# A decoder trunk's gated convolution: its input projection in pairs of weight tiles, 7 block products in place of 8

## The chip, the cores and the metric

The kernel runs on one core of a Trainium2 chip. The metric is device time in microseconds, the median of three runs. The engines are named as in the profile: PE (TensorE, matrix products), ACT (ScalarE), DVE (VectorE), POOL (GpSimd) and SP (SyncE, which here issues most of the loads). SBUF is the on-chip memory of 128 partitions; PSUM holds the banks into which PE writes its products, and PE reads only SBUF.

## The reference

One inference step of a trunk of four layers (attention, RG-LRU, gated convolution, attention), each followed by a SwiGLU feed-forward part (FFN). All arithmetic is float32, on 512 prompt tokens and 8 x 8 sample tokens, with a model width of 1024. The part that the change touches is the mixer of the third layer:

```python
def sconv_mixer(h, buf, w_in, conv_w, w_out):        # h = rmsnorm(x, gain)
    bcx = h @ w_in                                   # 1024 -> 3 * 1024
    bg, cg, xv = bcx[..., :D], bcx[..., D:2*D], bcx[..., 2*D:]
    y, new_buf = causal_dwconv(cg * xv, buf, conv_w) # 3 taps along the tokens, per channel
    return (bg * y) @ w_out, new_buf
def rmsnorm(x, g):
    return x * lax.rsqrt(jnp.mean(x * x, axis=-1, keepdims=True) + EPS) * g
def swiglu(h, wg, wu, wd):
    return (jax.nn.silu(h @ wg) * (h @ wu)) @ wd
```

## The kernel before

The tokens lie in two groups g = 0, 1 of 288 columns (256 prompt, 32 sample). x, h and mid are tiles of 8 chunks of 128 channels by 288 tokens for each group. A weight tile is 1024 x 128 and makes one chunk of 128 outputs. For float32 exactness each operand is held as a rounded high part and a remainder (hh and hl, wh and wl, mh and ml), and a product of one 128-channel chunk is three matmuls of 288 columns: hh with wh, hl with wh, hh with wl (mm3, lines 439 to 441). A unit is one weight tile times one group: 8 chunks, 24 matmuls. ACT makes wh from the raw tile (a cast), DVE makes wl (a subtraction), in wprep (lines 359 and 361), out of 4 raw buffers into 6 slots.

A Python scheduler (class Sched) with a cost for each operation fixes the order of the instructions on each engine when the program is built. Each engine then works through its own list in that order, and waits where an operand is not there yet. The cost table has one price for each operation, whatever runs beside it.

The mixers multiply h = x * gain (gsplit, line 473) and bring the norm's factor r in when the product leaves PSUM, so PE can start on a chunk of x as soon as it is there. In the gated convolution cg_evac multiplies by r squared (line 1237), the taps' result is multiplied by r (line 1261). For each of 8 chunks c the tiles cg, xv and bg follow one another, each for both groups: 24 tiles, 48 units. xv_evac forms cg * xv into ext (lines 1247, 1249), POOL writes the halos (halos, lines 1017 to 1023), conv does the three taps on DVE (lines 1038 to 1048), bg_evac multiplies by bg and splits the result into mh and ml (lines 468, 470).

The FFN already does its first projection in another way, from its fourth tile pair on (quad, inside ffn): gate and up tile of a pair, each cut in two halves along the inner axis, and the two token groups form a 2 x 2 block product, done with 7 products of half a tile (12 matmuls each) in place of 8. For that h must be exactly normed (hsplit, line 486, after the norm's factor is known), sums of the four token blocks (T1 to T4, tsums) are made once for the layer, and for each pair four sums of weight halves S1 to S4 (qsums, lines 378 to 388) - on DVE for the first NEAR = 2 pairs of a layer, on POOL after that. Each of the 7 half tiles gets its cast on ACT (line 412) and its subtraction on DVE (line 414). The product banks are partly reused: ACT copies a bank out (snap) before the next product is accumulated into it, and DVE adds the copy to another bank (lines 1343, 1380).

Of the kernel before, what the change touches and what calls it, by code (L numbers as in the profile page):

```python
# [8 lines left out]
F32 = mybir.dt.float32  # L9
# [4 lines left out]
P = 128  # L14
D = 1024
# [22 lines left out]
NEAR = 2  # L38
NSTP = 1
# [214 lines left out]
class Builder(Sched):  # L254
# [136 lines left out]
    def qprep(self, i):  # L391
        layer, last = self.quads[i]
# [89 lines left out]
    def hsplit(self, g, m, idx):  # L482

        hh, hl = (t[:, m, :] for t in self.h[g])
        keep = g == 1 or m < KC // 2
        if g == 0 and keep:
            yield ("wait", [("ffnlp", idx // 2)])
# [115 lines left out]
    def rstd(self, g, idx, ps, w1):  # L603
# [14 lines left out]
        if idx % 2:  # L618
# [591 lines left out]

    def sconv(self, layer):
        nc = self.nc
# [4 lines left out]
        def enter():  # L1217
            self.open(layer)
            lt = self.lt
            cr = lt("cr", [P, 384])  # L1220
            nc.gpsimd.dma_start(out=cr, in_=self.a["cr"])
            st["sst"] = self.pick(cr, CR, "sst")
# [3 lines left out]
            st["ext"] = Pool([(lt(f"ext{i}", [P, w]), lt(f"cv{i}", [P, w])) for i in range(3)])  # L1226
            st["u"] = Pool([lt(f"u{i}", [P, N]) for i in range(8)])
            st["r2"] = [lt(f"rr{g}", [P, N]) for g in range(2)]

        def cg_evac(g, c, ps):  # L1230
            [t] = yield ("acq", st["u"], 1)
            yield ("wait", [("r", g, idx)])
            if c == 0:
                yield ("D", cD(N, 1))
                nc.vector.tensor_mul(st["r2"][g], self.rt[g], self.rt[g])
            yield ("D", cD(N, 1))
            nc.vector.tensor_mul(t, ps[:, :N], st["r2"][g])
# [4 lines left out]
        def xv_evac(g, c, ps):  # L1242
# [4 lines left out]
            nc.vector.tensor_mul(ext[:, 2:2 + NP], u[:, :NP], ps[:, :NP])  # L1247
            yield ("D", cD(NS))
            nc.vector.tensor_mul(self.sview(ext, S0, SS)[:, :, 2:SS], u[:, NP:].rearrange("p (b t) -> p b t", t=T),
                                 ps[:, NP:N].rearrange("p (b t) -> p b t", t=T))  # L1250
            yield ("free", self.pp, [ps])
# [8 lines left out]
            yield ("D", cD(N))  # L1260
            nc.vector.tensor_mul(u, u, self.rt[g])
            yield ("set", ("cu", g, c))

        def bg_evac(g, c, ps):
# [3 lines left out]
            nc.vector.tensor_mul(u, u, ps[:, :N])  # L1268
            yield ("free", self.pp, [ps])
# [4 lines left out]

        self.hook(6, enter)
        for c in range(KC):
            for ev in (cg_evac, xv_evac, bg_evac):
                i = self.take()
                for g in range(2):
                    self.add(g, lambda prio, i=i, g=g, c=c, ev=ev: self.unit(  # L1280
                        i, g, self.h, self.hkeys(g, idx), lambda ps: ev(g, c, ps)))
        self.mixed = [("mc", g, c) for g in range(2) for c in range(KC)] + [("out", layer)]
# [9 lines left out]
    def ffn(self, layer):  # L1292
# [6 lines left out]
        hk = KC // 2  # L1299
        T = {}  # L1300
        mixed = self.mixed

        def enter():
            yield ("wait", mixed)
            self.open(f"{layer}f")
            for n in ("T2", "T1", "T3", "T4"):
                T[n] = tuple(self.lt(n + s, [P, hk, N], F32R) for s in "hl")
            self.stp = Pool([tuple(self.lt(f"S{j}{i}", [P, HW]) for j in range(2)) for i in range(NSTP)])
            self.b11 = [self.lt(f"b11{i}", [P, N]) for i in range(hk)]
            self.qseen = []  # L1310
            yield ("set", ("ffnlp", layer))

        def tsums(k):
            yield ("wait", [("h", g, idx, m) for g in range(2) for m in (k, k + hk)])
            b11, b12, b22 = (self.whole.pop(gm) for gm in ((0, k), (1, k), (1, k + hk)))
            hh, hl = (a[:, k + hk, :].bitcast(F32) for a in self.h[0])
            [t4] = yield ("acq", self.scr, 1)
            sub, add = nc.vector.tensor_sub, nc.vector.tensor_add
            for n, t, x, y, op in (("T1", b11, b12, b11, sub), ("T3", b12, b22, b12, sub), ("T2", b22, b22, b11, sub),
                                   (None, t4, hh, b22, sub), ("T4", t4, t4, hl, add)):  # L1320
                yield ("D", cD(N))
                op(t, x, y)

            def parts(n, t):
                yield from self.split(T[n][0][:, k, :], T[n][1][:, k, :], t, N, 1)
            for n, t in (("T1", b11), ("T3", b12), ("T2", b22), ("T4", t4)):
                yield ("spawn", parts(n, t), None, [("T", layer, n, k)])
            yield ("wait", [("T", layer, n, k) for n in ("T1", "T3", "T2", "T4")])
            yield ("free", self.scr, [b12, b22, t4])
# [23 lines left out]
        def quad(i, s, m, lst):  # L1353
            key = lambda g: (layer, s, g, m)
            h = lambda g, z: [a[:, z * hk:(z + 1) * hk, :] for a in self.h[g]]
            hkeys = lambda g, z: [("h", g, idx, m) for m in range(z * hk, (z + 1) * hk)]
            tkeys = lambda n: [("T", layer, n, k) for k in range(hk)]
            add = nc.vector.tensor_add
            c = {}

            def prod(n, ps, x, first, last):
                slot, wh, wl = self.qh.pop((i, n))
                yield ("P", 0.369 * hk, None, None, 864 * hk)
                xh, xl = x
                mm = nc.tensor.matmul
                for k in range(hk):
                    mm(ps[:, :N], lhsT=wh[:, k, :], rhs=xh[:, k, :], start=first and k == 0, stop=False, skip_group_check=not first)  # L1367
                    mm(ps[:, :N], lhsT=wh[:, k, :], rhs=xl[:, k, :], start=False, stop=False, skip_group_check=not first)  # L1368
                    mm(ps[:, :N], lhsT=wl[:, k, :], rhs=xh[:, k, :], start=False, stop=k == hk - 1, skip_group_check=not first)  # L1369
                yield from self.usehalf(slot)  # L1370

            def snap(n, ps):
                [c[n]] = yield ("acq", self.scr, 1)
                yield ("A", cA(N))
                nc.scalar.copy(c[n], ps[:, :N])
                yield ("set", ("c", i, n))

            def plus(t, ps):
                yield ("D", cD(N))
                add(t, t, ps[:, :N])  # L1380

            def silu(t):
                yield ("A", cA(N, 1), None, "silu")
                nc.scalar.activation(out=t, in_=t, func=AF.Silu)  # L1384

            def gate0():
                yield ("wait", [("c", i, 1)])
                yield from plus(c[1], b)
                yield ("free", self.pp, [b])
                yield from silu(c[1])  # L1390
                yield ("set", ("gs", i))

            def up1():
                yield ("wait", [("c", i, 5)])
                yield from plus(c[5], a)
                yield ("set", ("u", i))

            def gate1():
                yield from plus(c[2], d)
                yield ("free", self.pp, [d])  # L1400
                yield from silu(c[2])
                yield ("wait", [("u", i)])
                yield ("D", cD(N))
                nc.vector.tensor_mul(c[2], c[2], c[5])
                yield ("free", self.scr, [c[5]])
                yield from done(1, key(1), m, c[2])

            yield ("wait", [("qw", i, "A11")] + hkeys(0, 0))
            [a] = yield ("acq", self.pp, 1)
            yield from prod("A11", a, h(0, 0), True, False)  # L1410
            yield ("spawn", snap(1, a), None, [])
            yield ("wait", [("qw", i, "A12")] + hkeys(0, 1))
            [b] = yield ("acq", self.pp, 1)
            yield from prod("A12", b, h(0, 1), True, True)
            yield ("spawn", gate0(), None, [])
# [260 lines left out]
```

## Time and profile before

| | |
|---|---|
| median of 3 runs | 2353.8 us (2353.73 to 2353.94) |
| the profiled execution | 2353.24 us; its span, first to last instruction, is 2351.3 us |
| granted TensorE clock, mean | 0.998 |
| PE busy | 2324.0 us, 99% of the span |
| DVE busy | 1672.2 us, 71% |
| ACT busy | 1226.6 us, 52% |
| POOL busy | 542.6 us, 23% |

A row of the timeline has the start (us from the span's start), the duration, engine, line, operation and operands, and in brackets the idle time before it with what ended it. Consecutive instructions of one engine overlap a little in such records, so the cost of one in a full queue is read from start to start. The gated convolution's mixer stands between 1161 us (the norm's matmul of group 0 before it) and 1363 us (that of the FFN behind it).

### The profile page before, as it was taken

What the parts mean: (1) busy time and instruction counts of PE and PEld (TensorE: products, weight loads), DVE (VectorE), ACT (ScalarE), POOL (GpSimd) and SP (SyncE); (2) the same over time, 40 slices, a digit from 0 to 9 for tenths busy, and PEclk for the clock granted to TensorE, in tenths of its full rate; (3) what the DMA queues carried; (4) which work ended last, traced back from release to release, by engine and by line L of the source; (5) the groups of instructions that cost most, each with busy time, mean ns of one, the idle gap of its engine ahead of it and who ended that gap; (6) DMA issues with size and microseconds to landing.
All of it is one profiled execution on the core that took longest, in us unless ns stands there. A gap on an engine that the chain in (4) does not pass through costs nothing.

```text
span 2351.3 us, 44296 instructions
## 1 busy us (share of the span) xinstructions
PE 2324.0 (99%) x17596; PEld 2295.5 (98%) x17596; DVE 1672.2 (71%) x3315; ACT 1226.6 (52%) x2545; POOL 542.6 (23%) x636
## 2 busy tenths in 40 slices
PE   9999999999999999999999999999999999999998
PEld 8899999999999999999999999999999899999998
DVE  8978848486886885848665578484868959757474
ACT  8955625255695653525422256252548945535353
POOL 2300334240231033323000003242402400333330
PEclk9999999999999999999999999999999999999999
DMA  5111323233222132323322213232242111323131
GB/s 189 61 57 47 112 87 99 73 101 102 72 82 93 52 122 66 113 72 101 97 85 82 83 55 98 93 98 81 88 138 83 56 46 54 126 73 110 62 109 49
DMA packets 64064, 203.69 MB, mean 87 GB/s; under 512 B 11041, under 2 KB 13905, under 8 KB 63841
## 3 DMA queue, kind: packets, MB, share of 16 engines
q1 hardware_dynamic: 62800, 199.52, 26.7%
q8 instruction: 138, 2.26, 0.4%
q10 hardware_dynamic: 720, 0.73, 0.1%
q0 software_dynamic: 336, 0.61, 0.1%
q14 instruction: 70, 0.57, 0.1%
HBM read 197.87 MB, written 4.94 MB: 86 GB/s over the span
## 4 chain that ended last, share of the span: by engine, by line
PE 86%; ACT 6%; DVE 4%; issue 2%; DMA 1%; POOL 0%; DVEq 0%; ACTq 0%
PE bank L439 16%; PE bank L440 16%; PE bank L441 16%; PE bank L1367 12%; PE bank L1369 12%; PE bank L1368 12%; ACT s L753 2%; ACT wh L359 1%; DVE P L841 1%; PE bank L890 1%; PE bank L906 1%; ACT P L847 0%; DVE P L855 0%; ACT PT L892 0%; DVE wl L361 0%
## 5 line engine op out<-in xcount | busy, mean ns | idle before, releaser
L439 PE MATMUL bank<-mh,wh 128*128 128x288 f32 x1984 | 589.2, 297 | 1.7 <-ACT mh L468 1.7
L440 PE MATMUL bank<-ml,wh 128*128 128x288 f32 x1984 | 586.0, 295 | 0.5 <-DVE ml L470 0.4
L441 PE MATMUL bank<-mh,wl 128*128 128x288 f32 x1984 | 583.7, 294 | 0.0
L439 PE MATMUL bank<-hh,wh 128*128 128x288 f32 x1344 | 404.1, 301 | 4.1 <-ACT s L1123 1.5
L440 PE MATMUL bank<-hl,wh 128*128 128x288 f32 x1344 | 397.3, 296 | 0.0
L441 PE MATMUL bank<-hh,wl 128*128 128x288 f32 x1344 | 396.3, 295 | 0.0
L414 DVE TENSOR_TENSOR wl<-raw,wh 128x512 fp32r<-128x512 f32 x380 | 375.9, 1011 | 22.8 <-ACT wh L412 22.6
L359 ACT CAST wh<-raw 128x1024 fp32r<-128x1024 f32 (+2 forms) x217 | 219.0, 1014 | 326.0 <-PE bank L440 213.1
L439 PEld LDWEIGHTS bank<-mh,wh 128*128 128x128 f32 x1984 | 371.9, 187 | 3.4 <-ACT mh L468 2.5
L440 PEld LDWEIGHTS bank<-ml,wh 128*128 128x128 f32 x1984 | 372.5, 188 | 1.8 <-DVE ml L470 1.3
L441 PEld LDWEIGHTS bank<-mh,wl 128*128 128x128 f32 x1984 | 373.7, 188 | 0.0
L361 DVE TENSOR_TENSOR wl<-raw,wh 128x1024 fp32r<-128x1024 f32 (+2 forms) x217 | 256.7, 1183 | 65.9 <-ACT wh L359 64.0
L655 DVE TENSOR_TENSOR x<-bank,x 128x288 f32<-128x288 f32 x224 | 101.9, 457 | 280.1 <-PE bank L441 279.9
L412 ACT CAST wh<-raw 128x512 fp32r<-128x512 f32 x380 | 229.5, 619 | 95.2 <-PE bank L440 94.6
L1367 PE MATMUL bank<-hh,wh 128*128 128x288 f32 x912 | 270.0, 296 | 0.0
L1368 PE MATMUL bank<-hl,wh 128*128 128x288 f32 x912 | 269.1, 295 | 0.0
L1369 PE MATMUL bank<-hh,wl 128*128 128x288 f32 x912 | 268.2, 294 | 0.0
L439 PEld LDWEIGHTS bank<-hh,wh 128*128 128x128 f32 x1344 | 252.5, 188 | 6.7 <-ACT s L1123 1.7
L440 PEld LDWEIGHTS bank<-hl,wh 128*128 128x128 f32 x1344 | 253.1, 188 | 0.8
L441 PEld LDWEIGHTS bank<-hh,wl 128*128 128x128 f32 x1344 | 253.7, 189 | 0.1
L1384 ACT ACTIVATE s<-s 128x288 f32<-128x288 f32 x152 | 67.8, 446 | 216.7 <-DVE s L1380 215.6
L1369 PEld LDWEIGHTS bank<-hh,wl 128*128 128x128 f32 x912 | 171.9, 188 | 0.0
(382 smaller groups left out, 4863.9 us busy)
## 6 DMA issues: line engine op xcount, KB each, us to landing
raw<-in_w SPq DMA_DIRECT2D x303, 512.0 KB
raw<-in_w SPq DMA_DIRECT2D x64, 448.0 KB
out_y<-x SPq DMA_DIRECT2D x12, 144.0 KB
x<-in_x SPq DMA_DIRECT2D x4, 288.0 KB
x<-in_x SPq DMA_DIRECT2D x2, 576.0 KB
ck<-in_ckt SPq DMA_DIRECT2D x4, 256.0 KB
cv<-in_cv SPq DMA_DIRECT2D x4, 256.0 KB
ca<-in_ca SPq DMA_DIRECT2D x2, 480.0 KB
```

The source lines that it names most:

```text
L359: self.nc.scalar.copy(fh[:, z], r[:, z])
L361: self.nc.vector.tensor_sub(fl[:, z], r[:, z], fh[:, z].bitcast(F32))
L412: self.nc.scalar.copy(fh, src)
L414: self.nc.vector.tensor_sub(fl, src, fh.bitcast(F32))
L439: mm(out, lhsT=wh(k), rhs=xh(k), start=(k == 0), stop=False)
L440: mm(out, lhsT=wh(k), rhs=xl(k), start=False, stop=False)
L441: mm(out, lhsT=wl(k), rhs=xh(k), start=False, stop=(k == n - 1))
L655: nc.vector.tensor_add(x[:, m, :], ps[:, :N], x[:, m, :])
L1367: mm(ps[:, :N], lhsT=wh[:, k, :], rhs=xh[:, k, :], start=first and k == 0, stop=False, skip_group_check=not first)
L1368: mm(ps[:, :N], lhsT=wh[:, k, :], rhs=xl[:, k, :], start=False, stop=False, skip_group_check=not first)
L1369: mm(ps[:, :N], lhsT=wl[:, k, :], rhs=xh[:, k, :], start=False, stop=k == hk - 1, skip_group_check=not first)
L1384: nc.scalar.activation(out=t, in_=t, func=AF.Silu)
```

## The change

Only the gated convolution layer changes. x is exactly normed before its projection (hsplit in place of gsplit; BLOCKED names the norms that do this), so that r and r squared go out of the evacuations. The first two chunks stay as units (the copy out of PSUM for cg is now on ACT). From the third chunk on two tiles that share their inputs are taken as a pair: (cg, xv) of a chunk, and the bg tiles of two chunks (S_ORDER; the packed weights are reordered to match). Each such pair is a quad of 7 products; there are 9. The FFN's quad, tsums and the tiles T1 to T4 become methods that both use, with what is done with the four results handed in: for (cg, xv) the products and taps, for (bg, bg) the gating. The T1 tiles of this layer lie in chunks 6 and 7 of mid, which are needed last. Two pairs of ext buffers are there in place of three, and three u tiles in place of eight.

```diff
+BLOCKED = (1, 3, 4, 5, 7)
+SPRE = 2
+S_ORDER = []
+for _c in range(KC):
+    if _c < SPRE:
+        S_ORDER += [(1, _c), (2, _c), (0, _c)]
+    elif (_c - SPRE) % 2:
+        S_ORDER += [(1, _c - 1), (2, _c - 1), (1, _c), (2, _c), (0, _c - 1), (0, _c)]
...
-        if idx < 2 * self.layers and idx % 2 == 0:
+        if idx < 2 * self.layers and idx not in BLOCKED:
             yield ("spawn", self.gsplit(g, m, idx), GOFF, [("h", g, idx, m)])
...
-        if idx % 2:
+        if idx in BLOCKED:
             for m in range(KC):
                 yield ("spawn", self.hsplit(g, m, idx), GOFF + 0.01 * m, [("h", g, idx, m)])
...
+    def tsums(self, k, idx, done=None):        # moved out of ffn
...
+        for n, t, x, y, op in (("T1", b11, b12, b11, sub), ("T3", b12, b22, b12, sub), ("T2", b22, b22, b11, sub),
+                               (None, t4, hh, b22, sub), ("T4", t4, t4, hl, add)):
+            yield ("D", cD(N))
+            op(t, x, y)
...
+    def quad(self, i, lst, idx, dest, first, second):
...
+        def snap(n, ps):
+            [c[n]] = yield ("acq", self.scr, 1)
+            yield ("A", cA(N))
+            nc.scalar.copy(c[n], ps[:, :N])
+            yield ("set", ("c", i, n))
+
+        def head(g, n, ps):
+            t = yield from dest(g, c[n])
+            yield ("D", cD(N))
+            add(t, c[n], ps[:, :N])
...
+        def tail1():
+            yield ("wait", [("c", i, 5)])
+            yield ("D", cD(N))
+            add(c[5], c[5], a[:, :N])
+            yield ("set", ("u", i))
...
     def sconv(self, layer):
...
-            st["ext"] = Pool([(lt(f"ext{i}", [P, w]), lt(f"cv{i}", [P, w])) for i in range(3)])
-            st["u"] = Pool([lt(f"u{i}", [P, N]) for i in range(8)])
-            st["r2"] = [lt(f"rr{g}", [P, N]) for g in range(2)]
+            st["ext"] = Pool([(lt(f"ext{i}", [P, w]), lt(f"cv{i}", [P, w])) for i in range(2)])
+            st["u"] = Pool([lt(f"u{i}", [P, N]) for i in range(3)])
+            self.blocks(idx, [lambda k, s=s: self.mid[k // 2][s][:, KC - 2 + k % 2, :] for s in range(2)])
...
         def cg_evac(g, c, ps):
...
-            nc.vector.tensor_mul(t, ps[:, :N], st["r2"][g])
+            yield ("A", cA(N))
+            nc.scalar.copy(t, ps[:, :N])
...
             yield from self.conv(u, ext, t, 3, "scw", None, c)
             yield ("free", st["ext"], [(ext, t)])
-            yield ("D", cD(N))
-            nc.vector.tensor_mul(u, u, self.rt[g])
...
+            self.add_quad(i, lst, idx, not order, *(cgxv(c) if part else bgbg(c)))
```

On DVE, in the gated convolution: this is the piece between two weight tiles in the program before, for one chunk, with a group's taps (L1038 to L1048), the multiplication by r (L1261), the gating (L1268) and two whole-tile wl (L361). wl_80 and ext_2_11866 are buffers with their numbers.

```order
L1247 TENSOR_TENSOR ext_2_11866<-u_2_11868,bank_61 128x256
L1249 TENSOR_TENSOR ext_2_11866<-u_2_11868,bank_61 128x4x8
L361 TENSOR_TENSOR wl_80<-raw_71,wh_79 128x1024
L1038 TENSOR_SCALAR cv_2_11867<-ext_2_11866,cpack 128x296
L1042 SCALAR_TENSOR_TENSOR cv_2_11867<-ext_2_11866,cpack,cv_2_11867 128x296
L1046 SCALAR_TENSOR_TENSOR u_2_11868<-ext_2_11866,cpack,cv_2_11867 128x256
L1048 SCALAR_TENSOR_TENSOR u_2_11868<-ext_2_11866,cpack,cv_2_11867 128x32
L1261 TENSOR_TENSOR u_2_11868<-u_2_11868,rt_108 128x288
L1268 TENSOR_TENSOR u_2_11875<-u_2_11875,bank_62 128x288
L470 TENSOR_TENSOR ml_103<-u_2_11875,mh_102 128x288
L1268 TENSOR_TENSOR u_2_11868<-u_2_11868,bank_66 128x288
L361 TENSOR_TENSOR wl_76<-raw_72,wh_75 128x1024
```

The same place in the changed program, inside a (cg, xv) quad: half-tile wl (L422), the additions of bank and copy (L1299, L1314), and the taps of both groups (L1046 to L1056) drawn together.

```order
L422 TENSOR_TENSOR wl_84<-S_2_11875,wh_83 128x512
L1299 TENSOR_TENSOR u_2_11866<-s_94,bank_67 128x288
L1046 TENSOR_SCALAR cv_2_11863<-ext_2_11862,cpack 128x296
L1046 TENSOR_SCALAR cv_2_11865<-ext_2_11864,cpack 128x296
L1050 SCALAR_TENSOR_TENSOR cv_2_11863<-ext_2_11862,cpack,cv_2_11863 128x296
L1050 SCALAR_TENSOR_TENSOR cv_2_11865<-ext_2_11864,cpack,cv_2_11865 128x296
L1054 SCALAR_TENSOR_TENSOR u_2_11867<-ext_2_11862,cpack,cv_2_11863 128x256
L1056 SCALAR_TENSOR_TENSOR u_2_11867<-ext_2_11862,cpack,cv_2_11863 128x32
L1054 SCALAR_TENSOR_TENSOR u_2_11868<-ext_2_11864,cpack,cv_2_11865 128x256
L1056 SCALAR_TENSOR_TENSOR u_2_11868<-ext_2_11864,cpack,cv_2_11865 128x32
L422 TENSOR_TENSOR wl_80<-raw_70,wh_79 128x512
L1314 TENSOR_TENSOR s_85<-s_85,bank_61 128x288
```

Whole-tile subtractions have become half-tile ones between which the additions and the taps stand; the multiplication by r is gone.

On POOL, in the gated convolution before: the halos of two groups stand directly one behind the other, and nothing else is there.

```order
L1017 MEMSET ext_2_11866 128x2
L1018 COPY halo_11859<-ext_2_11866 128x2
L1022 COPY ext_2_11866<-cr_11857 128x4x2
L1023 COPY outs_11861<-ext_2_11866 128x8
L1020 COPY ext_2_11862<-halo_11859 128x2
```

And now: the four sums of weight halves of a pair (L386 to L396, with the scratch S and the raw tiles) stand between the halos of one chunk and the next.

```order
L386 TENSOR_TENSOR S_2_11875<-raw_70 128x512
L389 TENSOR_TENSOR S_2_11876<-S_2_11875,raw_69 128x512
L392 TENSOR_TENSOR raw_70<-raw_69,raw_70 128x512
L396 TENSOR_TENSOR raw_69<-raw_69,S_2_11876 128x512
L1025 MEMSET ext_2_11862 128x2
L1026 COPY halo_11859<-ext_2_11862 128x2
L1030 COPY ext_2_11862<-cr_11857 128x4x2
L1031 COPY outs_11861<-ext_2_11862 128x8
```

28 such sums (7 pairs of 4) have come to POOL; the first two pairs have theirs on DVE.

## Rows read from the trace of the kernel before

**Rows 1.** The page: busy time, share of the span and instructions of each engine
```profile
PE 2324.0 (99%) x17596; PEld 2295.5 (98%) x17596; DVE 1672.2 (71%) x3315; ACT 1226.6 (52%) x2545; POOL 542.6 (23%) x636
```
**Rows 2.** Windows: stretch, its length, busy us (instructions) of PE, PEld, DVE, ACT, POOL, clock, DMA
```profile
1163.00:1363.00 200.00, 200.00 (x1500) 199.90 (x1500) 114.04 (x228) 47.36 (x69) 10.31 (x65) 1.00 0.27 84
1390.00:1410.00 20.00, 20.00 (x152) 20.00 (x152) 19.21 (x47) 11.01 (x27) 0.00 (x0) 1.00 0.01 2
1543.00:1554.00 11.00, 11.00 (x85) 11.00 (x84) 10.02 (x15) 6.38 (x15) 5.96 (x4) 1.00 0.34 93
```
**Rows 3.** Timeline of PE in an FFN quad, two rows 48 matmuls apart
```profile
1099.82 0.30 PE L1367 MATMUL bank<-hh,wh 128*128 128x288 f32 x1
...
1106.22 0.30 PE L1367 MATMUL bank<-T3h_1f,wh 128*128 128x288 f32 x1
```
**Rows 4.** Timeline of PE and DVE at the norm before the gated convolution, group 0
```profile
1161.42 0.65 PE L600 MATMUL bank<-s,ones 128*128 128x288 f32 x2
...
1162.04 0.29 PE L440 MATMUL bank<-hl,wh 128*128 128x288 f32 x1
...
1163.02 0.46 DVE L613 SCALAR_TENSOR_TENSOR s<-bank,s 128x288 f32<-128x288 f32 x1 [1.23 <-ACT s L610]
```
**Rows 5.** Timeline of DVE in the FFN behind, while its T sums are made
```profile
1395.65 0.46 DVE L1322 TENSOR_TENSOR s<-s,b_2f 128x288 f32<-128x288 f32 x1
1396.14 0.46 DVE L1322 TENSOR_TENSOR s<-hh,s 128x288 f32<-128x288 f32 x1
...
1397.38 0.68 DVE L414 TENSOR_TENSOR wl<-raw,wh 128x512 fp32r<-128x512 f32 x1
1397.98 0.45 DVE L470 TENSOR_TENSOR T1l_2f<-b_2f,T1h_2f 128x288 fp32r<-128x288 f32 x1
1398.35 0.45 DVE L470 TENSOR_TENSOR T3l_2f<-s,T3h_2f 128x288 fp32r<-128x288 f32 x1
```
**Rows 6.** Timeline of DVE in the gated convolution: one group's product and taps, one whole-tile wl
```profile
1244.95 0.42 DVE L1247 TENSOR_TENSOR ext<-u,bank 128x256 f32<-128x256 f32 x1 [0.97 <-PE bank L441]
1245.29 0.18 DVE L1249 TENSOR_TENSOR ext<-u,bank 128x32 f32<-128x32 f32 x1
1245.79 0.38 DVE L1038 TENSOR_SCALAR cv<-ext,cpack 128x296 f32<-128x296 f32 x1 [0.31 <-POOL ext L1022]
...
1247.44 0.46 DVE L1261 TENSOR_TENSOR u<-u,rt 128x288 f32<-128x288 f32 x1
...
1249.15 1.23 DVE L361 TENSOR_TENSOR wl<-raw,wh 128x1024 fp32r<-128x1024 f32 x1 [0.48 <-ACT wh L359]
1250.29 0.37 DVE L1038 TENSOR_SCALAR cv<-ext,cpack 128x296 f32<-128x296 f32 x1
```
**Rows 7.** Timeline of DVE and POOL in one FFN quad
```profile
1545.52 4.57 DVE L414 TENSOR_TENSOR wl<-raw,wh 128x512 fp32r<-128x512 f32 x3
1550.01 0.44 DVE L1380 TENSOR_TENSOR s<-s,bank 128x288 f32<-128x288 f32 x1
...
1553.44 1.15 DVE L414 TENSOR_TENSOR wl<-S_2f,wh 128x512 fp32r<-128x512 f32 x1
1554.52 0.82 DVE L470 TENSOR_TENSOR ml<-s,mh 128x288 fp32r<-128x288 f32 x2
...
1544.83 1.29 POOL L378 TENSOR_TENSOR S_2f<-raw 128x512 f32<-128x512 f32 x1 [1.97 <-DVE wl L414]
...
1552.67 1.38 POOL L388 TENSOR_TENSOR raw<-raw,S_2f 128x512 f32<-128x512 f32 x1 [3.13 <-DVE wl L414]
```
**Rows 8.** By source line: instructions, duration ns min/median/max, first and last start, forms
```profile
L414 DVE TENSOR_TENSOR wl<-raw,wh x380: 677/685/1802, 218.4 to 2278.1; 128x512 fp32r<-128x512 f32 x190
...
L748 DVE SCALAR_TENSOR_TENSOR s<-s,cpack,cos x36: 497/514/987, 25.6 to 1878.6; 128x288 f32<-128x288 f32 x36
```
**Rows 9.** Timeline of DVE and POOL in the first attention layer
```profile
57.88 0.98 DVE L748 SCALAR_TENSOR_TENSOR s<-s,cpack,cos 128x288 f32<-128x288 f32 x1
...
57.68 0.86 POOL L830 TENSOR_TENSOR ml<-s,ml 64x256 fp32r<-64x256 f32 x1
```

More of the change, by code (lines that the diff above doesn't have):

```diff
@@ L391, in qprep @@
     def qprep(self, i):
-        layer, last = self.quads[i]
+        last = self.quads[i][1]
         for j, n in enumerate(("A11", "A12", "S2", "S1", "S3", "S4", "A22")):
@@ L486, in hsplit @@
         if g == 0 and keep:
-            yield ("wait", [("ffnlp", idx // 2)])
+            yield ("wait", [("lpq", idx)])
             t = self.b11[m]
@@ L1209, in rglru, with blocks @@
         self.spawn(outputs(), 1e6, 0.0, [("out", layer)])
+    def blocks(self, idx, t1=None):
+        hk = KC // 2
+        T = self.T = {}
+        for n in ("T2", "T1", "T3", "T4"):
+            if n == "T1" and t1 is not None:
+                T[n] = t1
+            else:
+                T[n] = [lambda k, t=self.lt(n + s, [P, hk, N], F32R): t[:, k, :] for s in "hl"]
+        self.stp = Pool([tuple(self.lt(f"S{j}{i}", [P, HW]) for j in range(2)) for i in range(NSTP)])
+        self.b11 = [self.lt(f"b11{i}", [P, N]) for i in range(hk)]
+        self.qseen = []
+        self.set(("lpq", idx), 0.0)
@@ L1267, in bg_evac @@
             yield ("D", cD(N))
-            nc.vector.tensor_mul(u, u, ps[:, :N])
-            yield ("free", self.pp, [ps])
+            nc.vector.tensor_mul(u, u, x)
+            if ps is not None:
+                yield ("free", self.pp, [ps])
+            if c >= KC - 2:
+                yield ("wait", [("pd", st["last"], "S1")])
             mh, ml = self.mid[g]
@@ L1273, in bg_evac, with cgxv, dest, first @@
             yield ("set", ("mc", g, c))
-        self.hook(6, enter)
-        for c in range(KC):
-            for ev in (cg_evac, xv_evac, bg_evac):
+        def cgxv(c):
+            def dest(g, t):
+                [u] = yield ("acq", st["u"], 1)
+                return u
+            def first(g, t):
+                st["cg", g, c] = t
+                yield ("set", ("cg", g, c))
+            def second(g, t, x, ps=None):
+                yield from xv_evac(g, c, x, ps)
+            return dest, first, second
+        def bgbg(c):
+            def dest(g, t):
+                return t
+                yield
+            def first(g, t):
+                yield ("spawn", one(g, t), None, [])
+            def one(g, t):
+                yield from bg_evac(g, c, t)
+                yield ("free", self.scr, [t])
+            def second(g, t, x, ps=None):
+                yield from bg_evac(g, c + 1, x, ps)
+            return dest, first, second
+        self.hook(6, enter)
+        tprio = self.nunits[1] + TOFF
+        lst = 0
+        order = list(S_ORDER)
+        while order:
+            part, c = order[0]
+            if c < SPRE:
+                order.pop(0)
                 i = self.take()
+                ev = (lambda g, c, ps: bg_evac(g, c, ps[:, :N], ps), cg_evac,
+                      lambda g, c, ps: xv_evac(g, c, ps[:, :N], ps))[part]
                 for g in range(2):
@@ L1281, in sconv @@
                         i, g, self.h, self.hkeys(g, idx), lambda ps: ev(g, c, ps)))
+                continue
+            order = order[2:]
+            i = self.take()
+            self.take()
+            st["last"] = i
+            self.add_quad(i, lst, idx, not order, *(cgxv(c) if part else bgbg(c)))
+            lst ^= 1
         self.mixed = [("mc", g, c) for g in range(2) for c in range(KC)] + [("out", layer)]
@@ L1305, in enter, with silu @@
             self.open(f"{layer}f")
[L1306 to L1329, printed above, removed]
+            self.blocks(idx)
+        def silu(t, x):
+            yield ("A", cA(N, 1), None, "silu")
+            nc.scalar.activation(out=t, in_=x, func=AF.Silu)
         def gate_evac(g, key, ps):
             [t] = yield ("acq", self.scr, 1)
-            yield ("A", cA(N), None, "silu")
-            nc.scalar.activation(out=t, in_=ps[:, :N], func=AF.Silu)
+            yield from silu(t, ps[:, :N])
             yield ("free", self.pp, [ps])
@@ L1351, in done @@
             yield ("set", ("mf",) + key)
[L1353 to L1415, printed above, removed]
-            yield ("wait", [("qw", i, "S2"), ("c", i, 1)] + tkeys("T2"))
-            yield from prod("S2", a, T["T2"], False, False)
-            yield ("spawn", snap(2, a), None, [])
-            yield ("wait", [("qw", i, "S1")] + tkeys("T1"))
-            [d] = yield ("acq", self.pp, 1)
-            yield from prod("S1", d, T["T1"], True, False)
-            yield ("spawn", snap(5, d), None, [])
-            yield ("wait", [("qw", i, "S3"), ("c", i, 2)] + tkeys("T3"))
-            yield from prod("S3", a, T["T3"], False, False)
-            yield ("spawn", up1(), None, [])
-            yield ("wait", [("qw", i, "S4"), ("c", i, 5)] + hkeys(1, 1))
-            yield from prod("S4", d, h(1, 1), False, True)
-            yield ("spawn", gate1(), None, [])
-            yield ("wait", [("qw", i, "A22"), ("u", i)] + tkeys("T4"))
-            yield from prod("A22", a, T["T4"], False, True)
-            self.open_quads -= 1
-            self.next_unit(lst, self.t["P"])
-            yield ("wait", [("gs", i)])
-            yield ("D", cD(N))
-            nc.vector.tensor_mul(c[1], c[1], a[:, :N])
-            yield ("free", self.pp, [a])
-            yield from done(0, key(0), m, c[1])
@@ L1439, in start_quad, with pair, dest, first @@
-        def start_quad(prio, i, s, m, lst):
-            self.open_quads += 1
-            return quad(i, s, m, lst)
+        def pair(s, m):
+            def dest(g, t):
+                return t
+                yield
+            def first(g, t):
+                yield from silu(t, t)
+            def second(g, t, x, ps=None):
+                yield from times(g, (layer, s, g, m), m, t, x, ps)
+            return dest, first, second
         self.spawn(enter(), 0.0, 0.0)
-        for k in range(hk):
-            self.spawn(tsums(k), self.nunits[1] + TOFF + 0.1 * k, 0.0)
+        for k in range(KC // 2):
+            self.spawn(self.tsums(k, idx), self.nunits[1] + TOFF + 0.1 * k, 0.0)
@@ L1457, in ffn @@
                     continue
-                self.quads[i] = (layer, m == ns - 1)
-                lst = (m - pre) % 2
-                self.units[lst].append((i + QOFF, lambda prio, i=i, s=s, m=m, lst=lst: start_quad(prio, i, s, m, lst)))
-                for g in range(2):
-                    self.nunits[g] += 2
+                self.add_quad(i, (m - pre) % 2, idx, m == ns - 1, *pair(s, m))
             last = s == len(SEGS) - 1
@@ L1549, in _weights @@
             w = i["sconv_w_in"][0]
-            for c in range(8):
-                out += [_mt(w, _cols(8 + c)), _mt(w, _cols(16 + c)), _mt(w, _cols(c))]
+            out += [_mt(w, _cols(8 * part + c)) for part, c in S_ORDER]
             out += [_mt(i["sconv_w_out"][0], _cols(m)) for m in range(8)]
```

124 lines of the change are left out of this document (102 added, 22 removed).

## The prediction

> **What bounds the kernel now.** I read the page first: PE is busy 99% of the span, DVE 71%, POOL 23% [rows 1]. That is an average, so I went on to windows over the gated convolution's mixer, from one norm to the next: in 200 us PE is never idle, DVE is busy 114 us and POOL 10 us [rows 2]. No wait of PE stands there, so matmuls taken out of this stretch shorten the run one for one, as long as the other engines keep up. The timeline of PE gives the price: 48 matmuls from 1099.82 to 1106.22, so 0.1333 us each, inside an FFN quad as in a unit [rows 3]. The other two windows show what DVE looks like where the trick is already used: 19.21 of 20 us while the FFN norms h and makes its T sums, 10.02 of 11 us in a quad, PE full in both [rows 2]. So DVE is the engine to count. In a full queue one DVE instruction follows the other before the record of the first ends: a 128x288 one costs 0.37 us, a half-tile wl 0.60, a dependent one behind another 0.49 [rows 5]; a whole-tile wl 1.14 [rows 6].
>
> **The change part by part.**
>
> *PE.* 9 quads take 84 matmuls where 4 units took 96: 108 matmuls less, 14.4 us. That is the whole gain if PE stays full: 2338.8 from the profiled execution's 2353.24 us.
>
> *The later start of h.* The projection now waits for the norm. PE fills the time with the last out-products of group 1: in the new order 63 matmuls (8.4 us) stand between the norm's matmul and the first product with hh of group 0. From that matmul DVE needs 1.6 us to reach the norm's first instruction [rows 4], then some 9 us to the eighth chunk (two norm instructions, a whole-tile wl, eight products of 0.43, which lies between the 0.37 and 0.49 of rows 5, eight remainders of 0.37, two others). The first chunk is there after about 6 us, the eighth at about 10.6, and PE asks for it 84 matmuls (11.2 us) after the norm. It fits; I cost it at nothing. Without that cover it would be about 2 us once.
>
> *DVE, the sum that decides.* In the new order PE has 1108 matmuls from group 0's norm to the first out-product: 147.7 us. Two norm matmuls cost 0.35 us extra each (0.62 us from rows 4 less two of 0.1333). The first out-product needs chunk 7 of mid only at its 22nd matmul, 2.8 us in. Less 0.2 us for the hand-over, DVE has 151.0 us. In that time it has to do, in its order: 63 half-tile wl x 0.605 = 38.1; 48 remainders (h, T, mid) x 0.37 = 17.8; 20 T sums x 0.45 = 9.0 (some dependent, some not); 16 normings x 0.43 = 6.9; 27 additions of a copy and a bank x 0.37 = 10.0; 16 products cg * xv x 0.44 = 7.0 (0.34 to the second part [rows 6] and 0.10 for that); taps of 16 chunks, 4 alone x 1.65 [rows 6] and 12 drawn together, where the three dependent waits of 0.12 (0.49 less 0.37) go away, x 1.29: 22.1; 16 gatings x 0.37 = 5.9; 5 whole-tile wl for the out-projection x 1.14 = 5.7; the weight sums of the first two pairs, 8 x 0.62 = 5.0; some 3.9 for two norms and the end of the last adds. Sum 131.4 us, with the 1.6 us of the start 133.0. By that DVE would be done 18 us early, and this is also what an order with one fixed price for each operation assumes.
>
> *What the fixed price leaves out.* In the FFN quad three wl take 4.49 us from start to start of what follows, in place of 1.82, and one takes 1.08 in place of 0.60: together 3.1 us more in a quad, just while POOL makes that quad's four sums [rows 7]. So a POOL sum costs DVE 0.79 us there. The longest wl is 1802 ns against a median of 685 [rows 8]: 1.12 us is the price of one full collision. An addition that reads a bank is not stretched (0.44 us beside the sums) [rows 7]. In the FFN quad the sums fall partly into DVE's idle time and beside those additions. In the gated convolution's quads there is hardly idle time, and the taps are no cover either: L748, which like a tap has two tiles in SBUF, takes 0.98 us beside a POOL sum, its median is 0.51 [rows 8, 9]. Only the additions and half of the products read PSUM, about 5 of 24 instructions of a quad. 28 sums have come to POOL. No row shows a sum beside a full DVE: the bounds are 0 (every sum beside something that reads PSUM) and 28 x 1.12 = 31.4 us. I take 0.92 each, between the quad's 0.79 and the full 1.12: 25.8 us.
>
> The Trainium skill, page "SBUF — State Buffer", section "Who interferes with whom", says that a DVE instruction with two SBUF inputs and a GpSimd instruction that reads SBUF exclude each other, and that the second waits for the whole of the first. The trace agrees for wl and for L748. Taken strictly, the rule gives about 1.1 us for each sum, a loss some 5 us above mine, and 2356.
>
> *Small waits of DVE.* POOL's halos now stand behind sums of 1.3 to 1.4 us [rows 7], the taps wait for the halos, the remainders for ACT's casts. In the dense 20 us of the FFN 0.8 us were idle [rows 2], 4%. Over 150 us that would be 6; part of it is in the sum already (dependent spacing). I take 4, bounds 0 and 12.
>
> *The sum.* 133.0 + 25.8 + 4 = 162.8 us of DVE against 151.0: PE loses 11.8 us of the 14.4 to waits for wl and for the last ml. Net 2.6 us faster than the profiled execution, 2350.6; the median of the runs stood 0.6 above it, so 2351.2.
>
> *What costs nothing.* ACT has 88 more rows in its order, copies and half-tile casts; from 47 us busy in 200 [rows 2] it goes to some 90 in 148, below DVE. The r products that go (16 of 0.37 and 18 that leave or go to ACT) are already missing from the list above. SP loads the same bytes. After the out-products begin DVE has only 51 us of PE work with 3 more whole-tile wl and the adds beside it, so nothing is carried into the FFN.
>
> **The rivals.**
>
> *PE stays full.* If the sums cost DVE at most 0.5 us each (14 us), DVE needs 133.0 + 14 + 2 = 149 us and PE loses nothing: 2353.24 - 14.4 + 0.6 = 2339.4. At the quad's 0.79 (22 us) and 2 us of small waits the loss is 6 us, and the time 2345.5. For it: the FFN's quads run at 10 of 11 us with PE full [rows 2]. Against it: the (cg, xv) quad has 4.6 us of additions, products and taps besides its 4.2 us of wl; with 3 to 4 us of collisions that is about 12.3 in PE's 11.2.
>
> *Slower.* Each collision costs the full 1.12 (31.4 us), and because POOL, itself held up, delivers halos and sums late, DVE waits 12 us more: 133.0 + 31.4 + 12 = 176 us, a loss of 25, so 2353.24 + 11 + 0.6 = 2365. It turns slower than before from a loss of 14.4 us on, that is from 32.4 us of collisions and waits together; I have 29.8. For it: POOL's queue now mixes short urgent copies with sums. Against it: the order leaves 2 to 4 us of other DVE work between a product in ext and its taps.
>
> *The change brings no fewer products.* Excluded: the new order has 108 matmuls less, and rows 3 show the same pace in a quad.
>
> **How the numbers follow.** A run tells 0.2%, 4.7 us, from no change: faster is below 2349.1, slower above 2358.5. The forecast is DVE as the limit with a loss of 10 to 19 us, within the 0.2% (2349 to 2358): 0.42. PE full or nearly so, a loss up to 10 us: 0.34. Slower, a loss beyond 19: 0.24. The predicted time is 2351.2, in the middle of what 0.79 to 1.12 us per sum give with 2 to 6 us of small waits (2345 to 2359). The range leaves out the two ends, full PE and the worst queueing: 2341 to 2361.
>
> **What would show it.** Right: the quads of this layer show PE waiting for wl by DVE, mostly from the third pair on, DVE above 9.5 of 10 us there, wl beside POOL sums at 1.1 to 1.8 us, and 10 to 14 us idle in PE. The start: no PE wait between norm and first product with hh. Wrong: PE without idle time in the quads (then the collisions hide beside the taps, and L1050 or L1054 show no stretch); or DVE idle for more than 10 us waiting on POOL or ACT; or PE waiting for ACT's copies of banks, which I have at nothing.

## The result, and the profile after

The changed kernel takes 2369.6 us (2368.3 to 2370.7), the one before 2353.8 (2353.0 to 2353.9): ratio 1.0068, interval 1.0055 to 1.0080. It is 15.8 us slower; 2351.2 was predicted, in a range of 2341 to 2361. The 108 matmuls and their 14.4 us are gone, so some 30 us were lost. From the FFN's norm behind the layer to the end both kernels take 988 us, so the loss stands in the changed layer.

The page, and the windows from the norm's matmul of group 0 to the last product with h (in the kernel before such a stretch is the first window of [rows 2]). Columns as there.

```profile
PE 2320.1 (98%) x17488; PEld 2288.1 (97%) x17488; DVE 1726.1 (73%) x3413; ACT 1257.9 (53%) x2637; POOL 586.6 (25%) x664
```
```profile
1159.24:1338.30 179.06, 159.56 (x1115) 156.36 (x1113) 152.38 (x307) 73.26 (x158) 54.89 (x93) 0.94 0.21 63
...
1290.65:1295.40 4.75, 4.75 (x24) 4.75 (x25) 1.98 (x5) 0.00 (x0) 0.00 (x0) 0.64 0.43 117
```

PE, full before, is idle for 19.5 of these 179 us, and the mean clock is 0.94. But DVE is not full either: 152.4 us busy, 26.7 idle. In the old kernel such idle time of DVE was harmless; here two engines wait for each other. The views of waits show for what (who waited <- for whom, us in total, times, longest):

```profile
PE bank L1286 <- DVE wl L422: 18.6, 7, 4.5
PE bank L448 <- DVE hl L478: 0.6, 2, 0.3
PE bank L447 <- ACT hh L476: 0.3, 1, 0.3
...
DVE s L1314 <- PE bank L1286: 8.7, 7, 1.7
DVE s L1299 <- PE bank L1286: 5.3, 5, 1.5
DVE u L1299 <- PE bank L1286: 3.7, 4, 1.7
DVE b L1299 <- PE bank L1286: 3.2, 3, 1.5
DVE x L663 <- PE bank L449: 2.0, 2, 1.3
DVE wl L422 <- ACT wh L420: 1.3, 2, 1.1
...
DVE cv L1046 <- POOL ext L1030: 0.4, 2, 0.2
```

PE waits 18.6 us for wl in 7 waits; four of 3.1 to 4.6 us stand in the quads 3, 5, 6 and 8, each time at the first matmul that needs S3's wl (T3h with wl). DVE waits 20.9 us in 19 waits for a bank that PE has still to finish. For POOL's halos it hardly waits.

One of the four, the (bg, bg) quad, in the timelines of PE, DVE, ACT and POOL:

```profile
1285.68 0.29 PE L1284 MATMUL bank<-T3h,wh 128*128 128x288 f32 x1
1285.81 0.29 PE L1285 MATMUL bank<-T3l,wh 128*128 128x288 f32 x1
...
1290.65 0.45 PE L1286 MATMUL bank<-T3h,wl 128*128 128x288 f32 x1 [4.55 <-DVE wl L422]
1290.90 0.44 PE L1284 MATMUL bank<-T3h,wh 128*128 128x288 f32 x1
1291.14 0.44 PE L1285 MATMUL bank<-T3l,wh 128*128 128x288 f32 x1
```
```profile
1282.75 0.46 DVE L1299 TENSOR_TENSOR s<-s,bank 128x288 f32<-128x288 f32 x1 [1.55 <-PE bank L1286]
1283.12 0.70 DVE L422 TENSOR_TENSOR wl<-S,wh 128x512 fp32r<-128x512 f32 x1
1283.74 0.45 DVE L1409 TENSOR_TENSOR u<-u,s 128x288 f32<-128x288 f32 x1
1284.11 1.41 DVE L1046 TENSOR_SCALAR cv<-ext,cpack 128x296 f32<-128x296 f32 x1
1285.55 1.47 DVE L1050 SCALAR_TENSOR_TENSOR cv<-ext,cpack,cv 128x296 f32<-128x296 f32 x1
1286.94 1.38 DVE L1046 TENSOR_SCALAR cv<-ext,cpack 128x296 f32<-128x296 f32 x1
1288.24 0.47 DVE L1054 SCALAR_TENSOR_TENSOR u<-ext,cpack,cv 128x256 f32<-128x256 f32 x1
...
1289.91 0.68 DVE L422 TENSOR_TENSOR wl<-raw,wh 128x512 fp32r<-128x512 f32 x1
```
```profile
1281.89 0.62 ACT L420 CAST wh<-raw 128x512 fp32r<-128x512 f32 x1
...
1283.90 1.44 POOL L386 TENSOR_TENSOR S<-raw 128x512 f32<-128x512 f32 x1 [0.63 <-DVE wl L422]
1285.42 1.28 POOL L389 TENSOR_TENSOR S<-S,raw 128x512 f32<-128x512 f32 x1
1286.65 1.49 POOL L392 TENSOR_TENSOR raw<-raw,raw 128x512 f32<-128x512 f32 x1
```

Read from the top of DVE's list. It is early and stands idle 1.55 us before an addition whose bank PE has not finished; the cast of S3 is there at 1282.51, before DVE goes on, but its subtraction stands further back. First come the wl of S1, a gating, and the eight tap instructions of both groups, and only then the wl of S3, which PE wants at 1285.95. The same wl of S1 sets POOL going: it frees the one pair of scratch tiles S, and the next pair's three sums run back to back just beside the taps, where three of DVE's instructions take 1.38 to 1.47 us in place of 0.36 to 0.53. PE stops for 4.55 us, and its next 15 matmuls come 0.24 us apart, at a granted clock of 0.64 in the window above (the lower of the two levels, 1.2 GHz, for most of it). Behind the four stops the trace has 66 matmuls at that spacing, 0.107 us more each than in [rows 3]: 7.1 us.

### The profile page after: what moved, and what is told of

Read it like the earlier page. It is cut to its first block, busy times and chain, and to the rows that moved or that the text cites. A ratio compares the mean times of both kernels' runs of the same rounds, so it can differ in the third digit from the quotient of the medians.

```text
span 2368.6 us, 44341 instructions
## 1 busy us (share of the span) xinstructions
PE 2320.1 (98%) x17488; PEld 2288.1 (97%) x17488; DVE 1726.1 (73%) x3413; ACT 1257.9 (53%) x2637; POOL 586.6 (25%) x664
## 4 chain that ended last, share of the span: by engine, by line
PE 84%; ACT 7%; DVE 6%; issue 2%; POOL 0%; DMA 0%; DVEq 0%; ACTq 0%
PE bank L447 14%; PE bank L449 14%; PE bank L448 14%; PE bank L1284 13%; PE bank L1286 13%; PE bank L1285 13%; ACT s L761 2%; ACT wh L367 1%; DVE cv L1050 1%; PE bank L898 1%; DVE wl L369 1%; PE bank L914 1%; DVE wl L422 1%; DVE P L849 0%; ACT P L855 0%
## 5 line engine op out<-in xcount | busy, mean ns | idle before, releaser
L422 DVE TENSOR_TENSOR wl<-raw,wh 128x512 fp32r<-128x512 f32 x425 | 411.0, 987 | 24.2 <-ACT wh L420 24.0
L367 ACT CAST wh<-raw 128x1024 fp32r<-128x1024 f32 (+2 forms) x199 | 200.0, 1009 | 241.3 <-PE bank L448 156.4
L447 PE MATMUL bank<-hh,wh 128*128 128x288 f32 x1056 | 318.1, 301 | 4.4 <-ACT s L1131 1.5
L448 PE MATMUL bank<-hl,wh 128*128 128x288 f32 x1056 | 311.9, 295 | 0.6 <-DVE hl L478 0.6
L449 PE MATMUL bank<-hh,wl 128*128 128x288 f32 x1056 | 310.9, 294 | 0.0
L420 ACT CAST wh<-raw 128x512 fp32r<-128x512 f32 x425 | 255.3, 619 | 95.3 <-PE bank L448 94.7
L1284 PE MATMUL bank<-hh,wh 128*128 128x288 f32 x1020 | 303.7, 298 | 0.0
L1285 PE MATMUL bank<-hl,wh 128*128 128x288 f32 x1020 | 302.6, 297 | 0.0
L1286 PE MATMUL bank<-hh,wl 128*128 128x288 f32 x1020 | 301.6, 296 | 0.2 <-DVE wl L422 0.2
L369 DVE TENSOR_TENSOR wl<-raw,wh 128x1024 fp32r<-128x1024 f32 (+2 forms) x199 | 235.4, 1183 | 53.4 <-ACT wh L367 51.3
L447 PEld LDWEIGHTS bank<-hh,wh 128*128 128x128 f32 x1056 | 198.1, 188 | 7.3 <-ACT s L1131 1.8
L448 PEld LDWEIGHTS bank<-hl,wh 128*128 128x128 f32 x1056 | 198.4, 188 | 1.7 <-DVE hl L478 1.0
L449 PEld LDWEIGHTS bank<-hh,wl 128*128 128x128 f32 x1056 | 198.7, 188 | 0.2 <-DVE wl L369 0.2
L1286 PEld LDWEIGHTS bank<-hh,wl 128*128 128x128 f32 x1020 | 193.8, 190 | 0.6 <-DVE wl L422 0.4
L1285 PEld LDWEIGHTS bank<-hl,wh 128*128 128x128 f32 x1020 | 193.2, 189 | 0.0
```

The source lines that it names most:

```text
L367: self.nc.scalar.copy(fh[:, z], r[:, z])
L369: self.nc.vector.tensor_sub(fl[:, z], r[:, z], fh[:, z].bitcast(F32))
L420: self.nc.scalar.copy(fh, src)
L422: self.nc.vector.tensor_sub(fl, src, fh.bitcast(F32))
L447: mm(out, lhsT=wh(k), rhs=xh(k), start=(k == 0), stop=False)
L448: mm(out, lhsT=wh(k), rhs=xl(k), start=False, stop=False)
```

## Experiments

Theory O: the order does it, DVE idle before an addition and then a block in front of the wl that PE needs. Theory C: the collisions with POOL's sums do it, as predicted, only larger. Of each experiment one number is also read in its trace: how DVE's time from the norm to the last product with h divides.

**a1, the taps ranked later.** In the scheduler a lower number goes first. With i the number of a pair's first weight tile, the wl of its S3 has i + 0.14 (L418); the taps inherit the rank of the quad two weight tiles earlier, i - 0.25. The expectation puts the stops at 23 us and the lower clock at 8.7; the views above give 19.5 and 7.1.

```diff
-            yield ("spawn", taps(g, c, u, ext, t), None, [("cu", g, c)])
+            yield ("spawn", taps(g, c, u, ext, t), 2.0, [("cu", g, c)])
```


> Same work as the changed kernel, all products and sums; only the taps get a lower rank in the scheduler (offset 2.0), so that on DVE the weight remainders of the following quad stand ahead of them. Theory O (order): PE loses its 23 us of stops and 8.7 us at the lower clock because the taps of both groups stand in DVE's list just ahead of the remainder for S3 that PE asks for next. Then the four stops of 3.4 to 4.8 us at the T3 products go, and with them the low clock behind them: 2344 to 2351 us. Theory C (collisions, as I predicted, only larger): DVE simply has too little time, since POOL's 28 sums hold it up; the same work in another order loses the same, with the stops elsewhere: 2364 to 2372.

Measured 2355.0 us, ratio to before 1.0008 (0.9999 to 1.0018): 14.6 us of the changed kernel's time are gone with the same work in another order. The windows' row:

```profile
1158.84:1322.90 164.06, 153.69 (x1115) 149.06 (x1114) 156.10 (x305) 73.34 (x156) 55.61 (x93) 1.00 0.23 71
```

DVE is busy 156.1 us, as before this edit and even a little more, but idle only 8.0 in place of 26.7, and the clock is whole. PE still loses time, now in many short stops of up to 1.5 us. O holds for this half. The time is 4 us above O's range, so O is not all.

**b1, the sums made narrow.** The order is unchanged.

```diff
+        m = HW if near or self.quads[i][0] != 4 else 16
-        pl.tensor_add(s1, u[:, :HW], u[:, HW:])
+        pl.tensor_add(s1[:, :m], u[:, :m], u[:, HW:HW + m])
```


> The changed kernel's order, instruction for instruction; POOL's 28 sums of weight halves in the gated convolution are made on 16 of 512 columns, so this layer's result is not the reference's. Theory C: without the sums nothing holds DVE up, the stops go altogether: 2338 to 2344 us, no stop over 0.5 us at the T3 products. Theory O: the taps still stand ahead of S3's remainder; only their stretch of some 2.5 to 3 us goes, so four stops of 1 to 2.2 us stay at the T3 products, too short to bring the clock down: 2346 to 2353.

Measured 2349.9 us, 0.9984 (0.9975 to 0.9994), 19.7 less than the changed kernel. DVE's row, and PE at the place shown above:

```profile
1159.23:1317.70 158.47, 151.39 (x1114) 148.82 (x1113) 132.44 (x307) 73.18 (x157) 23.69 (x93) 1.00 0.23 71
```
```profile
1277.77 0.40 PE L1287 MATMUL bank<-T3h,wl 128*128 128x288 f32 x1 [1.56 <-DVE wl L423]
1278.01 0.30 PE L1285 MATMUL bank<-T3h,wh 128*128 128x288 f32 x1
1278.15 0.30 PE L1286 MATMUL bank<-T3l,wh 128*128 128x288 f32 x1
```

DVE's busy time falls from 152.4 to 132.4 us; its idle time stays, 26.0. The four stops at T3 stay too, at 0.3 to 1.6 us, and behind them the clock is whole. So the width of the 28 sums costs 19.9 us of DVE, 0.71 each, and the end comes earlier by as much: PE is idle for 12.4 us less and busy for 8.2 us less, most of that the lower clock. But without the sums' width this order still takes 8.1 us more than a1's order without them (a2, below). O's expectation holds, C's fails.

**c1, the taps made narrow**, 16 columns in place of 256 to 296 (the last tap's part for the 32 sample columns stays), order and sums unchanged.

```diff
+        q, p = (16, 16) if kw == 3 else (n - kw + 1, NP)
-            v.tensor_scalar(out=t[:, :n - kw + 1], in0=ext[:, 0:n - kw + 1], scalar1=self.cst(w, c), scalar2=None,
+            v.tensor_scalar(out=t[:, :q], in0=ext[:, 0:q], scalar1=self.cst(w, c), scalar2=None,
```


> The changed kernel's order, instruction for instruction; the taps of the gated convolution are made on 16 columns in place of 256 to 296, so this layer's result is not the reference's. POOL's sums are whole. Theory O: what stood ahead of S3's remainder now takes some 0.1 us each, the stops at the T3 products go: 2341 to 2348 us. If the stops came from S3's cast on ACT, which stands behind a copy of a bank, or from POOL's halos (theory A), the four stops stay at 1.5 us or more: 2347 to 2356. Theory C: DVE has 20 us less to do, but 28 collisions with the remainders stay: 2343 to 2350, short stops spread over the quads.

Measured 2361.0 us, 1.0033 (1.0021 to 1.0045): only 8.6 less, and no theory had it. DVE, POOL, ACT (the cast of S3) and PE at the same place:

```profile
1279.33 1.27 DVE L1047 TENSOR_SCALAR cv<-ext,cpack 128x16 f32<-128x16 f32 x1
1280.63 1.32 DVE L1051 SCALAR_TENSOR_TENSOR cv<-ext,cpack,cv 128x16 f32<-128x16 f32 x1
1281.88 1.31 DVE L1047 TENSOR_SCALAR cv<-ext,cpack 128x16 f32<-128x16 f32 x1
1283.10 0.22 DVE L1055 SCALAR_TENSOR_TENSOR u<-ext,cpack,cv 128x16 f32<-128x16 f32 x1
...
1283.98 0.69 DVE L422 TENSOR_TENSOR wl<-raw,wh 128x512 fp32r<-128x512 f32 x1
```
```profile
1279.12 1.44 POOL L386 TENSOR_TENSOR S<-raw 128x512 f32<-128x512 f32 x1 [0.63 <-DVE wl L422]
1280.64 1.28 POOL L389 TENSOR_TENSOR S<-S,raw 128x512 f32<-128x512 f32 x1
1281.88 1.27 POOL L392 TENSOR_TENSOR raw<-raw,raw 128x512 f32<-128x512 f32 x1
...
1277.12 0.62 ACT L420 CAST wh<-raw 128x512 fp32r<-128x512 f32 x1
1284.72 0.40 PE L1287 MATMUL bank<-T3h,wl 128*128 128x288 f32 x1 [3.38 <-DVE wl L422]
```

A tap of 16 columns, 0.22 us when alone, takes as long as the sum beside it. Three sums in a row let three DVE instructions through in 3.8 us (1279.33 to 1283.10), however small these are. Stops of 1.8 to 3.4 us stay at T3. What a block of short instructions loses to a row of sums goes by their number, and the theories had counted its width. The stops stayed, as theory A (ACT's cast) had it, but not for its reason: what ends this stop is the wl at 1283.98, and the cast was done at 1277.74, before PE asked.

**d1, units only**, SPRE = 8: x exactly normed, T sums made, no quads.

> The changed kernel with all eight chunks as units: x exactly normed, T sums made (and not used), no quad, no weight sums, no product less. My prediction put the later start of h at nothing: 2353 to 2355 us. The trace of the changed kernel shows two short waits of 0.6 and 0.3 us at the first products with hh and hl: if the start costs what it shows, 2354.5 to 2356.

Measured 2354.9 us, 1.0008 (0.9998 to 1.0017). The middle is 1.5 us above before. That lies in both expectations, and the interval holds no change too, so the run does not decide between them. In the middle it is a twentieth of the loss.

**a2, a1 and b1 together.**

> Later taps (as in a1) and POOL's sums on 16 of 512 columns (as in b1; the layer's result is not the reference's). If a1's remaining loss is DVE's time under collisions (DVE was idle only 8 us of 164 there), DVE now needs 156 - 20 = 136 us of the 149 that PE has for it, PE runs full, and only the start of some 1.5 us stays: 2339 to 2343 us. If what a1 still loses is waits of DVE's list for PE or ACT, the time stays at 2348 to 2352.

Measured 2341.8 us, 0.9949 (0.9934 to 0.9963).

```profile
1159.41:1310.20 150.79, 149.89 (x1115) 148.69 (x1114) 131.78 (x305) 73.42 (x156) 22.92 (x93) 1.00 0.25 78
```

PE is full but for 0.9 us: 12.1 of the 14.4 us come out, and what is missing is about d1's start. With a1, b1 and a2 the two causes are told apart: in a1's order the sums cost 13.2 us of time, in the changed kernel's 19.7; the order costs 8.1 us without the sums and 14.6 with them. Neither is the whole loss, and 6.5 us appear only where both meet.

**f1, six quads** (a1 with SPRE = 4), **f2, first tap on ACT** (a1 with `nc.scalar.mul` for the first tap), **f3, both.**

```diff
-        yield ("D", cD(n / 2, 2))
+        if kw == 3:
+            yield ("A", cA(n, 0, 1))
+            self.nc.scalar.mul(t[:, :n - kw + 1], ext[:, 0:n - kw + 1], self.cst(w, c))
```


> Later taps, and the first four chunks as units: 6 quads in place of 9, 72 matmuls less (9.6 us), 16 sums on POOL in place of 28. Collision account (0.7 to 1.0 us of DVE for each sum, with DVE full): three quads ask 34.4 to 37.9 us of DVE where PE takes 33.6, so four quads with POOL sums lose 1 to 6 us, and with 1.5 us for the start 2346 to 2352 us. If the loss came only from the heap of T sums and h at the layer's start, quads this late lose nothing: 2344 to 2346.

> Nine quads, later taps, and the first tap of the three (a multiplication by a number per channel) made by ACT in place of DVE. Where DVE is the limit, 12 pairs of taps fewer give 0.3 us each without, and up to 1.0 us each with a POOL sum beside it: 4 to 12 us off a1's 2355, that is 2343 to 2351. If instead every hand-over to ACT makes DVE wait (taps wait for ACT, ACT's copies of banks stand in front), it stays at 2352 to 2358.

> Six quads, later taps, first tap on ACT. DVE's need for three quads falls by 4 first taps to 33.2 at most beside some 34 of PE: the quads run full, 2353.5 - 9.6 + 1.5 = 2345.4 us, 2344 to 2347. If collisions cost more than 1 us each where DVE is full, 2348 to 2351.

Measured 2353.9 (1.0000, 0.9990 to 1.0009), 2363.8 (1.0041, 1.0026 to 1.0056) and 2357.2 us (1.0014, 1.0004 to 1.0023): three misses. Two reasons show. In all three the last attention layer, between its norm of group 1 and the FFN's, takes 160 us in place of 154 before. On PE the order there is the same in all three and not a1's: by tile names another product stands in 309 of 1249 places (f3 against a1). The scheduler has put another layer in another order. Without these 6 us f1 would stand inside its expectation. And in f2 the layer itself is longer than in a1 although DVE has less to do:

```profile
1159.33:1325.80 166.47, 154.42 (x1114) 150.49 (x1113) 144.63 (x291) 80.67 (x174) 53.41 (x93) 0.99 0.22 69
...
1276.41 0.46 DVE L1305 TENSOR_TENSOR s<-s,bank 128x288 f32<-128x288 f32 x1 [1.55 <-PE bank L1292]
```

DVE is busy 144.6 us, 11.5 less than in a1, and idle 21.8, again before an addition whose bank isn't done. Work was taken off DVE, and in the new order its waits are back; that they ate the gain is read from this row and not tested.

**g1, f1 with the taps priced as beside sums** (1.6 times); **g2, six quads, later taps and all sums on DVE; g3, nine quads, later taps and all sums on DVE.**

```diff
-        near = len(self.qseen) < NEAR
+        near = len(self.qseen) < NEAR or self.quads[i][0] == 4
```


> As f1 (6 quads, later taps), with the second and third tap priced 1.6 times in the scheduler, as they are beside POOL's sums. In f1 the FFN's norm behind the layer stood 4.9 us earlier than before, and 6.0 us were lost again in the last attention layer, whose order the scheduler had put otherwise. Here that order is the one of before: 2353.8 - 4.9 - 0.5, that is 2347 to 2350 us. If the 6.0 us are no matter of the order there, 2352 to 2355 as f1.

> 6 quads, later taps, and all 24 sums of weight halves of this layer on DVE; POOL makes halos only. A sum costs DVE 0.62 us, against 0.7 to 0.9 us that a POOL sum took from it, so DVE has no more to do than in f1 and nothing stretches: the layer ends 5 to 7 us earlier than before, 2346 to 2350 us. If DVE's own sums stand in front of remainders that PE waits for, 2350 to 2354.

> Nine quads, later taps (a1), and all sums of this layer on DVE. With sums of 16 columns on POOL DVE was busy 132 us of 151; 28 sums of 0.62 make 149 us, just what PE leaves: by the sum alone 2342 to 2347 us. If DVE needs some idle time between (the same in-order list as in a1, where 156 us busy took 164), 2350 to 2357.

Measured 2345.2 us (0.9964, 0.9952 to 0.9977), 2344.6 (0.9963, 0.9951 to 0.9976) and 2348.1 (0.9978, 0.9968 to 0.9987). All three are faster than both kernels. g1 and g2 come out 1.8 and 1.4 us below the ranges expected, g3 between its two. The rows of g2 and g3:

```profile
1158.26:1313.40 155.14, 154.28 (x1150) 153.39 (x1149) 133.34 (x297) 67.04 (x136) 17.46 (x65) 1.00 0.24 75
```
```profile
1158.26:1315.20 156.94, 153.90 (x1115) 149.47 (x1113) 147.40 (x335) 73.63 (x158) 20.54 (x65) 1.00 0.23 73
```

In g2 PE is full but for the start. In g3 DVE is busy 147.4 us, 8.7 less than with the sums on POOL in a1: a sum on DVE costs less than the collision with the same sum on POOL. It is then 94% busy with 9.5 us idle, and PE stops for some of it. g1 also shows where f1's 6 us had been: its attention layer takes 154 us again, with 34 of 1249 places on PE other than in a1 in place of 309. Some 6 of the 8.7 us between f1 and g1 are therefore the order of a layer that the edit doesn't touch. Not every other order costs that: in g2 and g3 it differs from a1's too, and the layer takes 153.8 us.

## Why the prediction was wrong

**What bounds the kernel; the gain.** Right. The matmuls come 0.133 us apart in the new quads outside the stops, and a2 brought 12.1 us of the 14.4 out. That DVE is the engine to count was right too.

**The DVE sum.** Nearly right: 158.8 us of work predicted (133.0 and 25.8), 152.4 measured; without most of the sums' cost 132.4 against 133.0.

**The sums beside DVE.** Mis-sized by a little, on the safe side: 0.92 us each predicted, 0.71 measured (after against b1). In a1's order, where DVE is nearly full as the prediction had it, they cost 24.3 us (a1 against a2), 0.87 each. That the taps are no cover was right: L1046 and L1050 take 1.4 to 1.5 us beside a sum. An addition that reads a bank isn't stretched (0.45 us), as in [rows 7]. The rule of the Trainium skill (page "SBUF — State Buffer", section "Who interferes with whom") holds as a mechanism: in c1 a tap with two inputs in SBUF (L1051, 16 columns) that starts at 1306.13, just behind a sum of 1.29 us at 1306.04, takes 1.22 us, and 0.22 alone. It holds the other way round as well, and that lowers the mean: five of the 28 sums started just behind a wl and waited themselves, 1.67 to 1.72 us, while the wl took its usual 0.68 to 0.69. Other sums met an addition that reads a bank, or an idle DVE.

**The step that failed: "Small waits of DVE ... I take 4, bounds 0 and 12."** It was 26.7 us of idle time, 20.9 of them waits for PE's banks in the quads, which I hadn't on the list at all: I had named halos and ACT's casts, and these make 0.4 and 1.3 us. I took the 4% idle of the FFN's dense 20 us [rows 2] for a property of DVE. It belongs to that order. With it DVE took 152.4 + 26.7 = 179.1 us where the sum had 162.8 for nearly the same stretch: 16.3 of the 18.4 us by which the forecast was off. The POOL sums cost more time than the order did, but the sum had them, at more than they cost; the idle time it did not have. The sum compared DVE's total with PE's total over 150 us, as if DVE could work ahead through the layer and spend it later. It can't: additions wait for products of the same quad, and what could be done early stands behind them; this is read from the lists, and a1 tests its second half. So the account has to hold between one such addition and the next wl that PE needs, 3.2 us in the quad shown (1282.75 to 1285.95), where DVE had 7.8 us to do (to 1290.59). The claim that without collisions DVE would be done 18 us early fell with it: in b1 DVE is busy 132.4 us, and still idle for 26.0, and PE stops for 7.1. That the step was the order's idle time a1 shows: same work, idle time 8.0 us, together 164.1 us of DVE against the 162.8 of the sum, and 2355.0 us, inside the range that I had given.

**PE at the lower clock.** Not in the prediction: 7.1 us, only behind the four long stops. b1's stops of up to 1.6 us idle had none behind them.

**The start.** Costed at nothing; PE waited 0.9 us in three short waits, and d1 stands 1.5 us above before, with an interval that includes nothing.

**ACT at nothing.** Right: no product waits for a copy of a bank in the list of waits.

**The rivals.** The slower one (2365, chance 0.24) came nearest, and named the wrong wait: POOL late with halos. DVE waited for halos for 0.4 us; POOL's three sums in a row met the block of taps. Of the signs I gave, PE's waits for wl came as written. DVE above 9.5 of 10 us in the quads did not: it is at 6.5 to 8.8 in the windows of 10 us from 1235 to 1295. The sign against me, "DVE idle for more than 10 us waiting on POOL or ACT", did not come as written either: DVE was idle for longer than that, but for PE, which no sign of mine covered.

## What to carry to other kernels

An engine that is 85% busy over a stage can still be the limit when it works through a fixed list and waits in it for the engine that waits for it: add up the work between two such waits, not over the stage. Before moving work to another engine, see where its instructions will start (here behind the release of one scratch pair) and what stands beside them then. When an order is computed from prices, an edit that takes work away can bring back waits, or change a layer far behind it: read the timeline of the new order before believing the sum.

## What the runs showed of the hardware

A DVE instruction with operands in SBUF that meets a running POOL sum is not slowed in proportion: it waits for the sum to end, whatever its own size. A tap of 16 columns takes 1.27 to 1.32 us beside sums of 1.27 to 1.44 at the place shown, 0.22 alone; one of 296 columns up to 1.54, 0.36 to 0.53 alone; a half-tile wl up to 1.78, 0.68 alone. A sum that starts just behind a wl waits in turn, 1.67 to 1.72 us. This holds for TENSOR_SCALAR as well, which reads one tile and a number per partition (L1046: 0.36 alone, 1.38 beside). Making the same sum on DVE took 0.60 to 0.63 us from start to start (g2).
